# Attention in two layers of a decoder trunk: masks added, negated and reduced in one VectorE pass from PSUM into SBUF

## The chip, the core and the metric

The program runs on one core of one Trainium2 chip. A core has TensorE (PE: matmuls; PEld in the profile is its weight load), VectorE (DVE), ScalarE (ACT), GpSimd (POOL), and SyncE (SP), which here only issues DMAs. Each engine works through its own queue of instructions in order and waits on semaphores for the others. [...] The metric is device time in microseconds for one execution, the median over runs.

## What is computed

A trunk of two layers on a sequence of 1024 tokens with 1024 features, float32. Layer 0 mixes by sparse attention with 12 heads of 64 features, layer 1 by causal attention with a forget gate. Both attend with 4 more heads to 256 memory tokens, and both end with a gated convolutional feed-forward part. What matters here is the masked softmax:

```python
def masked_softmax(s, mask):
    s = jnp.where(mask, s, NEG)
    s = s - jnp.max(s, axis=-1, keepdims=True)
    e = jnp.exp(s) * mask
    return e / jnp.maximum(jnp.sum(e, axis=-1, keepdims=True), 1e-30)
```

In layer 0 each head takes three of them for every block of 128 queries: over 63 compressed keys (one for 32 tokens, every 16 tokens), over selected blocks of keys (16 of at most 16 blocks, so all of them, causally), and over a window of the last 512 keys:

```python
        p_cmp = masked_softmax(s, cmp_end[None, :] <= t[:, None])
...
        p = masked_softmax(s.reshape(B, G, HG, Q_BLOCK, n_top * L_SEL), m_sel)
...
        m_win = (s_pos[None, :] >= 0) & (s_pos[None, :] <= t[:, None]) & (t[:, None] - s_pos[None, :] < WINDOW)
        p = masked_softmax(s, m_win)
...
        return g[..., 0:1] * o_cmp + g[..., 1:2] * o_slc + g[..., 2:3] * o_win
```

In layer 1 each head takes one, over all keys up to its query. The memory heads have no mask.

## The kernel before

[...] The stages are: projections of layer 0 (to 185 us in the profile), attention of layer 0 (to 660 us), output projection, feed-forward and the projections that layer 1 needs (to about 1480 us), attention of layer 1 (to 1870 us), and again output projection and feed-forward.

**Units.** Attention goes unit by unit; a unit is one head and one half (c = 0 or 1) of the queries, four blocks of 128 (`ii` = 0 to 3, called rows here). Layer 0 has 24 such units and 8 of memory heads, layer 1 the same numbers. The selected branch and layer 1 take 128 x (4c + ii + 1) keys for a row (`causal`, line 934), so 128 to 512 columns in the first half and 640 to 1024 in the second; the window branch takes 128 to 512 in the first and 640 in the second. The 64 compressed columns are scored beside the window's (`joint`).

**One unit, engine by engine.**

- `score` (line 362, the matmuls at 385) takes a `psa` buffer, two PSUM banks or 1024 columns; there are two such buffers. A group of rows that fits in 1024 columns (`groups`) is scored at a time: for each row and each stretch of columns within a bank, two matmuls with the query block as weights. Then come the masks, also as matmuls: the weights are the identity (`identb`, bf16), the moving operand is a bf16 tile of 0 and -1e30, and PSUM adds it up. A row of the selected branch and of layer 1 has one such matmul, of 128 columns on the diagonal (`caub`). A row of the window branch has one of 192 columns (`wcb`: 128 on the diagonal and 64 compressed), and in the second half another of 128 columns at the window's far edge (`winb`).
- `maximum` (line 387) has DVE reduce each row from PSUM to its negated maximum in `stat` (line 402; 404 for the 64 compressed columns). Memory units have four equal rows and take one instruction (398).
- `exponent` (line 406) has ACT read the row from PSUM, add the negated maximum, take exp, write p to SBUF, and sum it up (418; 421 for the compressed columns, whose sum DVE takes later). p's buffer is taken here when a unit's first group comes. In layer 0 the buffers have one copy for each half and branch (`ps0`, `ps1`, `pw0`, `pw1`; `pc` has two), in layer 1 two. After it the `psa` buffer is free.
- `sums` and `clamp` (DVE 431, 433, 434; POOL 438) make the reciprocal; `normalise` scales p, by POOL in layer 0 (461, 463) and by DVE in layer 1 (465).
- Then come steps of up to four 128-wide blocks: PE transposes p into a `psb` bank (`turn_p`, 495), ACT copies the high part (`upper_p`, 506), DVE subtracts it to get the low part (`lower_p`, 509), and PE multiplies both with the values (`value`, 519). `psb` has four buffers, `pt`, the tile of the two parts, three.
- Matmuls of projections (lines 240 to 242) that later units need are put between.

**The order.** In layer 0 (`planned`, line 659) the order on every engine is made before the program is written: each piece of work is a task with an engine, a price in microseconds, tasks that it depends on, a priority, and the buffers that it takes and gives back (`Plan`, line 44). A list scheduler plays them through, and the order in which they start is the order in the queues. Priorities count in steps: transposes of step k have k, the score of a branch has the step that first needs it, less a lead of 5. The prices of a score, a maximum and an exponential are at lines 710 to 712:

```python
                        s_us += 2 * sum(map(self.columns, segs)) + 0.11 * len(br["spans"][ii][2])
                        m_us += 0.15 + 1.04e-3 * w + (0.22 if joint else 0)
                        e_us += 0.49 + 0.82e-3 * w + (0.33 if joint else 0)
```

The score takes a `psa`, and the exponential gives it back (line 718); the exponential also depends on the transposes that read the old contents of its p buffer (`old`, line 717). In layer 1 (`attention`, line 541) there is no such plan: the order comes from slots. In step k stand the maximum, then the transposes, the high part, the exponential, the low part, the normalisation, the next score and projections, each for work begun so many steps earlier.

Of the kernel before, what the change touches and what calls it, by code (L numbers as in the profile page):

```python
# [18 lines left out]
P = 128  # L19
D = 1024  # L20
S = 1024
NT = S // P
KT = D // P
CH = 512
# [4 lines left out]
NMEM = 256  # L29
# [97 lines left out]
class Trunk:  # L127
# [43 lines left out]
    def constants(self):  # L171
        nc, cp, a = self.nc, self.cp, self.a
        c = cp.tile([P, C_CAU], F32, name="consts")
        nc.sync.dma_start(c, a["consts"][:, 0:C_CAU])
        self.ident = c[:, C_ID:C_ID + P]
        self.rv = c[:, C_RV:C_RV + 1]
        self.identb = cp.tile([P, P], BF16, name="identb")
        nc.vector.tensor_copy(self.identb, self.ident)
        self.m_cau = cp.tile([P, P], BF16, name="caub")
        self.nhalf = c[:, C_NH:C_NH + 1]  # L180

    def masks(self, pool, keep):
# [3 lines left out]
        self.m_win = keep.tile([P, P], BF16, name="winb")  # L186
        nc.vector.tensor_copy(self.m_win, m[:, P:2 * P])

        self.m_wc = keep.tile([P, NT, 192], BF16, name="wcb")
        nc.vector.tensor_copy(self.m_wc[:, :, P:], m[:, 2 * P:].rearrange("p (t n) -> p t n", t=NT))  # L190
        nc.vector.tensor_copy(self.m_wc[:, :, 0:P], m[:, 0:P].rearrange("p (o n) -> p o n", o=1).to_broadcast([P, NT, P]))

    def gain(self, pool, row, bufs=1):
        g = self.sb(pool, [P, D], F32, "gb", bufs)
# [167 lines left out]
    def score(self, it):  # L362
        nc, br, s = self.nc, it["br"], self.psa()
        it["s"] = s
        for ii, o, n in it["grp"]:
            k0, k1, masks = br["spans"][ii]
            if "joint" in br:
                f, t0 = n - 192, k0 // P
                segs = [(o + f, o + n, lambda k: k[:, t0 + f // P, :])]
                if f:  # L370
                    segs.insert(0, (o, o + f, lambda k: k[:, t0:t0 + f // P, 0:P]))
            else:
                cuts = [o] + [b for b in (CH,) if o < b < o + n] + [o + n]
                segs = [(b0, b1, lambda k, b0=b0, b1=b1: k[:, k0 + b0 - o:k0 + b1 - o]) for b0, b1 in zip(cuts, cuts[1:])]
            mms = []
            for q, k in zip(br["q"], br["k"]):
                for b0, b1, at in segs:
                    rhs = at(k)
                    out = s[:, b0:b1] if len(rhs.shape) == 2 else s[:, b0:b1].rearrange("p (t n) -> p t n", n=P)
                    mms.append((b0 // CH, out, q[:, ii * P:(ii + 1) * P], rhs))  # L380
            for mo, mk in masks:
                mms.append(((o + mo) // CH, s[:, o + mo:o + mo + mk.shape[1]], self.identb, mk))
            banks = [b for b, *_ in mms]
            for i, (b, out, w, rhs) in enumerate(mms):
                nc.tensor.matmul(out, w, rhs, start=b not in banks[:i], stop=b not in banks[i + 1:])  # L385

    def maximum(self, ap, it):
        nc, br, s, grp = self.nc, it["br"], it["s"], it["grp"]
        u, joint = it["u"], br.get("joint")
        if it["first"]:  # L390
            if it["load"]:
                u["stat"] = self.sb(ap, [P, 3, 4 * len(u["branches"])], F32, "stat", 5)
            for i, b in enumerate(u["branches"]):
                b["stat"] = u["stat"][:, :, 4 * i:4 * i + 4]
        br["same"] = len({k1 - k0 for k0, k1, _ in br["spans"].values()}) == 1
        if br["same"] and len(grp) == 4:
            n = grp[0][2]
            nc.vector.reduce_max(br["stat"][:, 0, :], s[:, 0:4 * n].rearrange("p (i n) -> p i n", n=n), axis=AX.X, negate=True)
        else:
            for ii, o, n in grp:  # L400
                w = n - 64 if joint else n
                nc.vector.reduce_max(br["stat"][:, 0, ii:ii + 1], s[:, o:o + w], axis=AX.X, negate=True)  # L402
                if joint:
                    nc.vector.reduce_max(joint["stat"][:, 0, ii:ii + 1], s[:, o + w:o + n], axis=AX.X, negate=True)

    def exponent(self, ap, it):
        nc, br, s = self.nc, it["br"], it["s"]
        joint = br.get("joint")
        if it["first"]:
            for b in (br, joint) if joint else (br,):  # L410
                tag, width, bufs = b["p"]
                b["pa"], b["pt"], b["len"] = self.sb(ap, [P, width], F32, tag, bufs), {}, 0
        for ii, o, n in it["grp"]:
            w = n - 64 if joint else n
            p = br["pa"][:, br["len"]:br["len"] + w]
            br["pt"][ii] = p
            br["len"] += w
            nc.scalar.activation(p, s[:, o:o + w], AF.Exp, bias=br["stat"][:, 0, ii:ii + 1], accum_out=br["stat"][:, 1, ii:ii + 1])  # L418
            if joint:
                p = joint["pt"][ii] = joint["pa"][:, ii * 64:(ii + 1) * 64]  # L420
                nc.scalar.activation(p, s[:, o + w:o + n], AF.Exp, bias=joint["stat"][:, 0, ii:ii + 1])
                joint["len"] += 64
    def sums(self, u, i0, i1):

        nc, st = self.nc, u["stat"][:, :, 4 * i0:4 * i1]
# [233 lines left out]
    def planned(self, ap, l, od, units, works, spare, lead):  # L659
# [3 lines left out]
        pl, steps, users, oT, done = Plan(psa=2, psb=4, pt=self.n_pt, wr=3), [], {}, [], {}  # L663
# [9 lines left out]
        for w in works:  # L673
            prio = [(count + i) * n_fill / total for i in range(w["n"])]
# [8 lines left out]
        for k, u in enumerate(units):  # L683
            brs = u["branches"]
            scored = brs if len(brs) == 1 else brs[0:2]
            for br in brs:
                tag, _, bufs = br["p"]
                same = users.setdefault(tag, [])
# [7 lines left out]
            for i, br in enumerate(scored):  # L696
                due = min(st["k"] for st in u["steps"] if any(q[0] is br for q in st["ps"]))
                prio, joint, es = due - lead, br.get("joint"), []
                gs = self.groups(br)
                for j, g in enumerate(gs):  # L700
                    it = {"u": u, "br": br, "grp": g, "first": j == 0, "load": i == 0 and j == 0}
                    s_us = e_us = m_us = 0.0
                    for ii, o, n in g:
                        if joint:
                            segs = ([n - 192] if n > 192 else []) + [192]
                        else:
                            cuts = [o] + [b for b in (CH,) if o < b < o + n] + [o + n]
# [12 lines left out]
                i1 = len(brs) if br is scored[-1] else i + 1  # L720
                pool = br["on"] == "pool"
# [210 lines left out]

    @staticmethod
    def causal(c, mask):
        return {ii: (0, (c * 4 + ii + 1) * P, [((c * 4 + ii) * P, mask)]) for ii in range(4)}

    def mem_units(self, ap, qd, kv, tags, need, on):
        nc = self.nc
        kd, vd = kv
        for h in range(NMH):  # L940
            kv = {}
            for c in range(2):
                br = {"spans": {ii: (0, NMEM, []) for ii in range(4)}, "kb": P, "gate": None, "p": tags[c], "on": on}

                def load(h=h, c=c, br=br, kv=kv):
                    if c == 0:
# [243 lines left out]
    def units0(self, ap):  # L1190
        nc = self.nc
        t_s, t_w, t_c = [("ps0", 1280, 1), ("ps1", 3328, 1)], [("pw0", 1280, 1), ("pw1", 2560, 1)], ("pc", 256, 2)
        for g in range(NG):
            kk, vv = {}, {}
            vc = self.vc[:, g].rearrange("n s d -> n (s d)")
            for h in range(g * 6, g * 6 + 6):
                for c in range(2):
                    sp_c = {ii: (0, 64, []) for ii in range(4)}
                    sp_w = {}
                    for ii in range(4):  # L1200
                        i = c * 4 + ii
                        k0 = max(0, i - 4) * P
                        sp_w[ii] = (k0, (i + 1) * P, ([(0, self.m_win)] if i >= 4 else []) + [(i * P - k0, self.m_wc[:, i, :])])
# [757 lines left out]
```

## Time and profile before

| | us |
|---|---|
| median of three runs | 2640.01 |
| lowest, highest | 2638.92, 2644.44 |
| the profiled execution | 2646.97 |
| its span, first to last instruction | 2645.2 |
| stage of layer 0's attention in it | 185 to 660 |
| stage of layer 1's attention in it | 1480 to 1870 |

A row of grouped instructions reads: line, engine, operation, tile written <- tiles read, shapes, count | busy time in us, mean ns of one | idle time of the engine just before them, and what ended it. A row of the waits reads: who waited, the line and tile, whom for, us in total, times, longest. A row of windows reads: the stretch and its length, then for each engine its busy us and the count of its instructions, PE's granted clock as a share, the DMA share and the rate; asked for one line or tile, it counts only those instructions. A row of the timeline has start, duration, engine, line, operation, tiles, and the number of instructions merged in it; matmuls overlap, since a new one streams in while the last drains.

### The profile page before, as it was taken

What the parts mean: (1) busy time and instruction counts of PE and PEld (TensorE: products, weight loads), DVE (VectorE), ACT (ScalarE), POOL (GpSimd) and SP (SyncE); (2) the same over time, 40 slices, a digit from 0 to 9 for tenths busy, and PEclk for the clock granted to TensorE, in tenths of its full rate; (3) what the DMA queues carried; (4) which work ended last, traced back from release to release, by engine and by line L of the source; (5) the groups of instructions that cost most, each with busy time, mean ns of one, the idle gap of its engine ahead of it and who ended that gap; (6) DMA issues with size and microseconds to landing.
All of it is one profiled execution on the core that took longest, in us unless ns stands there. A gap on an engine that the chain in (4) does not pass through costs nothing.

```text
span 2645.2 us, 36064 instructions
## 1 busy us (share of the span) xinstructions
PE 2505.2 (95%) x12642; PEld 2074.6 (78%) x12642; DVE 1824.2 (69%) x2681; ACT 1333.6 (50%) x2553; POOL 833.2 (32%) x722
## 2 busy tenths in 40 slices
PE   7879999888999999998999999999899999998998
PEld 6768888676877888886888987787677888886886
DVE  5637776567376787877765467778466787787765
ACT  4427776677244444544454356657244544443443
POOL 1236544745143545543000000000123555454000
PEclk9989999899999999999999999999999999999999
DMA  8473233432422323337434556666532333337523
GB/s 240 137 210 100 81 91 109 115 106 81 147 88 84 104 95 104 108 133 268 134 123 132 157 176 190 188 176 179 196 112 68 104 111 101 96 105 264 189 89 119
DMA packets 302701, 357.72 MB, mean 135 GB/s; under 512 B 37960, under 2 KB 183224, under 8 KB 302520
## 3 DMA queue, kind: packets, MB, share of 16 engines
q1 hardware_dynamic: 302520, 355.41, 43.1%
q8 instruction: 100, 1.64, 0.3%
q14 instruction: 81, 0.66, 0.1%
HBM read 245.55 MB, written 109.78 MB: 134 GB/s over the span
## 4 chain that ended last, share of the span: by engine, by line
PE 74%; DVE 5%; DMA 5%; issue 4%; POOL 4%; ACT 3%; SPq 1%; POOLq 0%; ACTq 0%; DVEq 0%
PE psa L240 11%; PE psa L241 11%; PE psa L242 11%; PE psb L240 8%; PE psb L242 8%; PE psb L241 8%; PE psa L385 7%; PE psb L519 4%; PE psb L495 4%; POOL gs L1752 1%; DVE pt L509 1%; DMA hT<-in_w_down_dram 1%; ACT ps L418 1%; ACT pt L506 1%; DVE stat L402 1%
## 5 line engine op out<-in xcount | busy, mean ns | idle before, releaser
L165 ACT ACTIVATE wh<-wr 128x512 fp32r<-128x512 f32 (+2 forms) x240 | 181.9, 761 | 337.5 <-PE psb L242 143.8
L166 DVE TENSOR_TENSOR wl<-wr,wh 128x512 fp32r<-128x512 f32 (+2 forms) x232 | 223.1, 963 | 148.3 <-ACT wh L165 147.7
L1737 DVE SCALAR_TENSOR_TENSOR v<-u,cw,v 128x1023 f32<-128x1023 f32 (+1 forms) x176 | 273.2, 1552 | 68.7 <-ACT v L1735 68.5
L509 DVE TENSOR_TENSOR pt<-psb,pt 128x512 fp32r<-128x512 f32 (+2 forms) x380 | 245.4, 658 | 93.1 <-ACT pt L506 90.8
L506 ACT ACTIVATE pt<-psb 128x512 fp32r<-128x512 f32 (+2 forms) x380 | 216.8, 582 | 143.5 <-PE psb L495 97.2
L1735 ACT ACTIVATE v<-u,cw 128x1024 f32<-128x1024 f32 x88 | 109.6, 1245 | 310.3 <-DVE u L1724 283.5
L519 PE MATMUL psb<-pt,vv 128*128 128x512 f32 (+2 forms) x864 | 254.5, 372 | 4.0 <-ACT pt L506 2.2
L402 DVE TENSOR_REDUCE stat<-psa 128x1 f32<-128x640 f32 (+7 forms) x288 | 201.3, 717 | 77.8 <-PE psa L385 76.8
L240 PE MATMUL psa<-hT,wh 128*128 128x512 f32 x560 | 219.1, 392 | 5.3 <-DVE u L1698 5.3
L385 PE MATMUL psa<-kk,qq 128*128 128x512 f32 (+4 forms) x792 | 191.6, 356 | 32.2 <-DMA qq<-qd 13.3
L242 PE MATMUL psa<-hT,wl 128*128 128x512 f32 x560 | 218.5, 390 | 0.2 <-DVE wl L166 0.2
L241 PE MATMUL psa<-hT,wh 128*128 128x512 f32 x560 | 218.6, 390 | 0.0
L204 POOL TENSOR_TENSOR rs<-ss,consts 128x1 f32<-128x1 f32 x44 | 25.9, 592 | 505.0 <-DVE ss L202 366.9
L418 ACT ACTIVATE ps<-psa,stat 128x128 f32<-128x128 f32 (+2 forms) x224 | 156.1, 704 | 47.5 <-DVE stat L402 43.8
L385 PEld LDWEIGHTS psa<-kk,qq 128*128 128x128 f32 x792 | 130.7, 198 | 50.8 <-ACT ps L418 16.7
L1639 POOL TENSOR_TENSOR ws<-wr 128x512 f32<-128x512 f32 x44 | 77.5, 1761 | 294.8 <-DMA wr<-in_w_up_dram 187.5
L240 PE MATMUL psb<-hT,wh 128*128 128x512 f32 x384 | 159.6, 416 | 1.8 <-ACT wh L165 1.1
L519 PEld LDWEIGHTS psb<-pt,vv 128*128 128x128 f32 x864 | 147.1, 194 | 17.5 <-DVE pt L509 4.5
L240 PE MATMUL psb<-wh 128*128 128x512 f32 x352 | 139.4, 396 | 20.5 <-ACT wh L165 20.4
L495 PE MATMUL psb<-consts,ps 128*128 128x128 f32 x928 | 150.9, 279 | 6.7 <-POOL ps L463 3.8
L579 POOL TENSOR_TENSOR wr<-wr 128x512 f32<-128x512 f32 x16 | 20.9, 1314 | 424.6 <-DMA wr<-o 423.8
L242 PE MATMUL psb<-hT,wl 128*128 128x512 f32 x384 | 151.9, 396 | 1.1 <-POOL wl L166 1.1
(304 smaller groups left out, 6908.0 us busy)
## 6 DMA issues: line engine op xcount, KB each, us to landing
wr<-in_w_up_dram SPq DMA_DIRECT2D x88, 512.0 KB
wr<-gd SPq DMA_DIRECT2D x154, 256.0 KB
gd<-v SPq DMA_DIRECT2D x88, 256.0 KB
gd<-gs SPq DMA_DIRECT2D x66, 256.0 KB
o<-ob SPq DMA_DIRECT2D x128, 128.0 KB
wr<-o SPq DMA_DIRECT2D x32, 512.0 KB
hT<-in_w_down_dram SPq DMA_DIRECT2D x64, 256.0 KB
qd<-st SPq DMA_DIRECT2D x56, 256.0 KB
```

Of the source, the lines that this page charges most:

```text
L166: (low or nc.vector).tensor_tensor(lo, src, f32(hi), ALU.subtract)
L240: mm(out, lh, rh, start=first, stop=False, skip_group_check=more)
L241: mm(out, lh, rl, start=False, stop=False, skip_group_check=more)
L242: mm(out, ll, rh, start=False, stop=last, skip_group_check=more)
L385: nc.tensor.matmul(out, w, rhs, start=b not in banks[:i], stop=b not in banks[i + 1:])
L402: nc.vector.reduce_max(br["stat"][:, 0, ii:ii + 1], s[:, o:o + w], axis=AX.X, negate=True)
L418: nc.scalar.activation(p, s[:, o:o + w], AF.Exp, bias=br["stat"][:, 0, ii:ii + 1], accum_out=br["stat"][:, 1, ii:ii + 1])
L495: nc.tensor.transpose(tp[0:kb, x:x + P], br["pt"][ii][:, o:o + kb], self.ident)
L506: self.nc.scalar.activation(st["hi"], st["src"], AF.Copy)
L509: self.nc.vector.tensor_tensor(st["lo"], st["src"], f32(st["hi"]), ALU.subtract)
L519: self.nc.tensor.matmul(u["o"][:, iis[0] * P:iis[0] * P + w], br["v"](j), t[:, x:x + w], start=st["begin"] and first and i == 0, stop=st[" ...
L1737: nc.vector.scalar_tensor_tensor(v[:, d:], u[:, :S - d], cw[:, tap, i:i + 1], v[:, d:], ALU.mult, ALU.add)
```

## The change

1. **Masks leave PE.** `identb` is gone, and `score` writes no mask matmuls. The masks become wider bf16 tiles in SBUF, as wide as a row: `caub` is 1024 columns, 0 and then the diagonal block, and a row of n columns takes its last n; `winb` is 640 columns (far edge, 384 of 0, diagonal); a new `cmpb` holds 8 x 64 for the compressed keys. Together they take 512 bytes a partition more than before.
2. **The maximum becomes `lift`.** For a row with a mask, DVE's `tensor_tensor_reduce` reads the scores from PSUM and the mask from SBUF, writes -(s + mask) to p in SBUF, and keeps the minimum of what it writes in `stat`. That is the negated maximum as before. A row of the window branch has two of these, as it had two maxima. p's buffer is now taken here. Rows of memory units (mask `None`) stay as they were.
3. **The exponential works in SBUF, in place.** exp(-1 x p + stat), from p to p.
4. **The plan in layer 0.** The score's price loses 0.11 us for each mask. The maximum, at its old price, now depends on the readers of the old p and gives the `psa` back; the exponential depends on the maximum alone, at its old price. For memory units the exponential still gives `psa` back, but the dependence on the old p has moved to the maximum there too.

Layer 1's slots are untouched, but `maximum` and `exponent` are shared.

```diff
-        self.identb = cp.tile([P, P], BF16, name="identb")
-        nc.vector.tensor_copy(self.identb, self.ident)
-        self.m_cau = cp.tile([P, P], BF16, name="caub")
+        self.m_cau = cp.tile([P, S], BF16, name="caub")
+        nc.vector.memset(self.m_cau[:, :S - P], 0.0)
...
-        nc.vector.tensor_copy(self.m_cau, m[:, 0:P])
...
+        nc.vector.tensor_copy(self.m_cau[:, S - P:], m[:, 0:P])
+        self.m_win = keep.tile([P, 5 * P], BF16, name="winb")
+        nc.vector.memset(self.m_win[:, P:4 * P], 0.0)
...
+        self.m_cmp = keep.tile([P, NT, 64], BF16, name="cmpb")
...
-            for mo, mk in masks:
-                mms.append(((o + mo) // CH, s[:, o + mo:o + mo + mk.shape[1]], self.identb, mk))
...
+        if br["spans"][0][2] is None:
+            n = grp[0][2]
+            nc.vector.reduce_max(br["stat"][:, 0, :], s[:, 0:4 * n].rearrange("p (i n) -> p i n", n=n), axis=AX.X, negate=True)
+            return
+        for ii, o, n in grp:
+            w = n - 64 if joint else n
+            self.lift(br, ii, s[:, o:o + w])
+            if joint:
+                self.lift(joint, ii, s[:, o + w:o + n])
+
+    def lift(self, br, ii, s):
+        w = s.shape[1]
+        p = br["pt"][ii] = br["pa"][:, br["len"]:br["len"] + w]
+        br["len"] += w
+        self.nc.vector.tensor_tensor_reduce(p, s, br["spans"][ii][2], -1.0, 3e38, ALU.add, ALU.min, br["stat"][:, 0, ii:ii + 1])
...
-            nc.scalar.activation(p, s[:, o:o + w], AF.Exp, bias=br["stat"][:, 0, ii:ii + 1], accum_out=br["stat"][:, 1, ii:ii + 1])
...
+            nc.scalar.activation(p, p, AF.Exp, bias=st[:, 0, ii:ii + 1], scale=-1.0, accum_out=st[:, 1, ii:ii + 1])
...
-                        s_us += 2 * sum(map(self.columns, segs)) + 0.11 * len(br["spans"][ii][2])
+                        s_us += 2 * sum(map(self.columns, segs))
...
-                    m = pl.add("DVE", m_us, lambda it=it: self.maximum(ap, it), [s], prio)
                     old = [r for b in (br, joint) if b and b["before"] for r in reads[id(b["before"])]]
-                    es.append(pl.add("ACT", e_us, lambda it=it: self.exponent(ap, it), [m] + old, prio, (), ["psa"]))
+                    kept = br["spans"][0][2] is None
+                    m = pl.add("DVE", m_us, lambda it=it: self.maximum(ap, it), [s] + old, prio, (), () if kept else ["psa"])
+                    es.append(pl.add("ACT", e_us, lambda it=it: self.exponent(ap, it), [m], prio, (), ["psa"] if kept else ()))
```

More of the change, by code (lines that the diff above doesn't have):

```diff
@@ L365, in score @@
         for ii, o, n in it["grp"]:
-            k0, k1, masks = br["spans"][ii]
+            k0 = br["spans"][ii][0]
             if "joint" in br:
@@ L395, in maximum @@
         br["same"] = len({k1 - k0 for k0, k1, _ in br["spans"].values()}) == 1
[L396 to L408, printed above, removed]
         if it["first"]:
@@ L934, in causal @@
     def causal(c, mask):
-        return {ii: (0, (c * 4 + ii + 1) * P, [((c * 4 + ii) * P, mask)]) for ii in range(4)}
+        n = [(c * 4 + ii + 1) * P for ii in range(4)]
+        return {ii: (0, n[ii], mask[:, S - n[ii]:]) for ii in range(4)}
     def mem_units(self, ap, qd, kv, tags, need, on):
@@ L942, in mem_units @@
             for c in range(2):
-                br = {"spans": {ii: (0, NMEM, []) for ii in range(4)}, "kb": P, "gate": None, "p": tags[c], "on": on}
+                br = {"spans": {ii: (0, NMEM, None) for ii in range(4)}, "kb": P, "gate": None, "p": tags[c], "on": on}
                 def load(h=h, c=c, br=br, kv=kv):
@@ L1197, in units0 @@
                 for c in range(2):
-                    sp_c = {ii: (0, 64, []) for ii in range(4)}
+                    sp_c = {ii: (0, 64, self.m_cmp[:, c * 4 + ii, :]) for ii in range(4)}
                     sp_w = {}
```

29 lines of the change are left out of this document (16 added, 13 removed).

## The prediction

> **What bounds the kernel now.** I began with the page's first part, to see which engine is full.
>
> ```profile
> span 2645.2 us, 36064 instructions
> PE 2505.2 (95%) x12642; PEld 2074.6 (78%) x12642; DVE 1824.2 (69%) x2681; ACT 1333.6 (50%) x2553; POOL 833.2 (32%) x722
> ```
>
> TensorE (PE) is full over the whole span, VectorE (DVE) has a third of its time left. The change touches two stages only, so I asked for busy time by stretch: the attention of layer 0 runs from 185 to 660 us, that of layer 1 is at its steadiest from 1530 to 1830 us.
>
> ```profile
> core 0: us, PE busy (x) PEld busy (x) DVE busy (x) ACT busy (x) POOL busy (x), PEclk, DMA share, GB/s
> 185.00:230.00 45.00, 33.36 (x187) 26.61 (x187) 21.71 (x47) 21.89 (x54) 15.47 (x21) 0.81 0.50 123
> 230.00:480.00 250.00, 246.37 (x1616) 208.45 (x1615) 186.88 (x362) 186.21 (x467) 138.75 (x196) 1.00 0.33 92
> 480.00:660.00 180.00, 148.90 (x894) 118.08 (x894) 117.63 (x223) 124.96 (x321) 98.81 (x130) 0.92 0.38 104
> 1530.00:1830.00 300.00, 297.20 (x1665) 241.50 (x1664) 223.97 (x480) 187.61 (x474) 5.16 (x4) 1.00 0.64 182
> ```
>
> Two of these stretches are bound by PE: 230 to 480 us (246.37 of 250) and layer 1 (297.20 of 300). DVE is at 75% in both. From 185 to 230 and from 480 to 660 us PE works 182.3 of 225 us, so there it stops for others. The view of waits in layer 0 tells for whom, where scores are concerned:
>
> ```profile
> PE psa L385 <- ACT pc L421: 8.8, 9, 2.1
> PE psa L385 <- ACT ps L418: 8.1, 6, 2.2
> ACT pw L418 <- PE psb L495: 2.7, 1, 2.7
> ```
>
> PE stood 8.8 + 8.1 = 16.9 us before a score matmul because an exponential had not yet read a `psa` bank. The third row is the only time an exponential waited for the transposes that still read its output buffer.
>
> **The change, part by part.** *Masks leave PE.* 336 matmuls with `identb` as weights go, 240 in layer 0 and 96 in layer 1 (24 units of four rows).
>
> ```profile
> L385 PE MATMUL psa<-caub,identb x192: 219/230/330, 196.8 to 1851.5; 128*128 128x128 bf16 x192
> L385 PE MATMUL psa<-wcb,identb x96: 246/251/383, 203.0 to 658.3; 128*128 128x192 bf16 x96
> L385 PE MATMUL psa<-winb,identb x48: 229/230/233, 217.9 to 658.3; 128*128 128x128 bf16 x48
> ```
>
> Their 230 ns is latency in a pipelined array and not what they cost; the cost is read from start to start on PE's timeline in layer 1:
>
> ```profile
> 1786.91 0.39 PE L519 MATMUL psb<-pt,mv 128*128 128x512 f32 x1
> 1787.14 0.46 PE L385 MATMUL psa<-kk,qq 128*128 128x512 f32 x2
> ...
> 1788.60 0.23 PE L385 MATMUL psa<-caub,identb 128*128 128x128 bf16 x1
> 1788.64 0.47 PE L519 MATMUL psb<-pt,mv 128*128 128x512 f32 x1
> 1788.95 0.27 PE L495 MATMUL psb<-consts,ps 128*128 128x128 f32 x1
> ```
>
> The mask itself holds PE for 1788.64 - 1788.60 = 0.04 us. The 512 columns after it take 1788.95 - 1788.64 = 0.31 us, where the same matmul behind a long one takes 1787.14 - 1786.91 = 0.23 us: behind so short a matmul the next weights are not loaded in time. So a mask costs between 0.04 and 0.12 us. I take 0.11, near the upper end, because most masks are followed by a matmul that starts late in this way. They lie as follows (masks alone):
>
> ```profile
> 230.00:480.00 250.00, 28.12 (x137) 10.96 (x137) 0.00 (x0) 1.00 0.33 92
> 480.00:660.00 180.00, 17.44 (x80) 6.88 (x80) 0.00 (x0) 0.92 0.38 104
> 1530.00:1830.00 300.00, 19.32 (x84) 8.11 (x84) 0.00 (x0) 1.00 0.64 182
> ```
>
> In the full stretch of layer 0 that is 137 x 0.11 = 15.1 us (5.5 to 16.4), all of it on the path. The other 240 - 137 = 103 save 11.3 us of PE, but there PE is at 81% and waits on others; I credit a third, 3.8 us (0 to 11.3). Layer 1: 96 x 0.11 = 10.6 us (3.8 to 11.5).
>
> *The score banks come free earlier.* A bank was held until the exponentials had read it, now until VectorE has. The wait of 2.2 us in the rows above, engine by engine:
>
> ```profile
> 585.88 1.68 DVE L402 TENSOR_REDUCE stat<-psa 128x1 f32<-128x128 f32 x4 [1.81 <-PE psa L385]
> ...
> 587.33 0.19 ACT L418 ACTIVATION_READ_ACCUMULATOR ps<-psa,stat 128x1 f32 x1
> 587.42 0.47 ACT L418 ACTIVATE ps<-psa,stat 128x256 f32<-128x256 f32 x1
> ...
> 588.59 0.47 PE L385 MATMUL psa<-kk,qq 128*128 128x192 f32 x2 [2.22 <-ACT ps L418]
> ```
>
> All maxima of the four rows had ended by 585.88 + 1.68 = 587.56; PE was let go at 588.59. Released by VectorE it would have come at least 1.03 us sooner, about half of its 2.22. Half of 16.9 is 8.4 us (0 to 16.9).
>
> *The maximum becomes an add, a scale, a minimum and a write.* The instruction count of the maxima stays (288 in layer 0, 96 in layer 1; the memory units keep theirs); the new form reads PSUM and a mask, and writes p. The nearest rows in layer 0:
>
> ```profile
> L509 DVE TENSOR_TENSOR pt<-psb,pt 128x512 fp32r<-128x512 f32 x197 | 131.3, 682 | 43.2 <-ACT pt L506 42.6
> L402 DVE TENSOR_REDUCE stat<-psa 128x1 f32<-128x640 f32 x60 | 49.2, 821 | 26.9 <-PE psa L385 26.5
> L402 DVE TENSOR_REDUCE stat<-psa 128x1 f32<-128x512 f32 x24 | 16.3, 680 | 0.6 <-PE psa L385 0.6
> L402 DVE TENSOR_REDUCE stat<-psa 128x1 f32<-128x1024 f32 x12 | 14.6, 1220 | 6.0 <-PE psa L385 6.0
> L404 DVE TENSOR_REDUCE stat<-psa 128x1 f32<-128x64 f32 x96 | 20.5, 214 | 0.0
> L431 DVE RECIPROCAL stat<-stat 128x4 f32<-128x4 f32 x32 | 5.5, 173 | 11.6 <-ACT ps L418 7.3 <-ACT pm L418 4.3
> ```
>
> A two-input pass from PSUM and SBUF over 512 columns takes 682 ns, the reduction 680: the pass itself costs nothing more. What VectorE may need is a second step that brings the accumulator out. No such step of VectorE stands in the trace. Below, it is nothing; above, it is as long as the smallest VectorE row, 0.17 us. ScalarE's own accumulator read goes on after 587.42 - 587.33 = 0.09 us, and I take that. [...] With the read the sum is the one below, without it it would be 9.7 us lower still.
>
> Where the maxima are:
>
> ```profile
> 230.00:480.00 250.00, 76.04 (x109) 1.00 0.33 92
> 230.00:480.00 250.00, 11.99 (x56) 1.00 0.33 92
> ```
>
> 165 of the 288 lie in the full stretch: 165 x 0.09 = 14.9 us, DVE 186.9 + 14.9 = 201.7 us in 250 - 15.1 = 235, or 86%. PE still hides that, with thinner cover; I charge 4 us (0 to 15). The other 123 add 11.1 us in stretches that go by latency; a third on the path is 3.7 us. In layer 1, with one maximum for each mask, DVE comes to 223.97 + 84 x 0.09 = 231.5 of 290 us, 80%, hidden by PE; I charge 2 us.
>
> *The exponentials read SBUF.* Copies of 512 columns by ScalarE:
>
> ```profile
> L757 ACT ACTIVATE ob<-psb 128x512 f32<-128x512 f32 x31 | 18.5, 598 | 8.5 <-PE psb L519 5.7 <-DMA o<-ob 2.6
> L785 ACT ACTIVATE hT<-wr 128x512 fp32r<-128x512 f32 x14 | 8.7, 635 | 0.0
> ```
>
> SBUF costs 37 ns more. In the full stretch 165 x 0.037 = 6.1 us on an engine at 186 of 250: hidden by PE. Outside, 123 x 0.037 = 4.6, a third is 1.5 us; without its cover the first would be 6.1 more.
>
> *A wait moves.* p is now claimed by VectorE's pass instead of by the exponential, so the wait for the last transposes of the old p stands in VectorE's queue, ahead of the subtractions at L509 that PE's value matmuls need. The order in layer 0 knows this dependence, and today it is met once, 2.7 us: nothing in the sum, a rival below. The masks' own preparation at the start (a memset and casts in place of casts) is of the same few instructions under the projections: nothing.
>
> Sum: -15.1 - 3.8 - 8.4 + 4 + 3.7 + 1.5 in layer 0, -10.6 + 2 in layer 1: **-26.7 us**. The profiled execution took 2646.97 us (span 2645.2, and 1.8 around it), 7.0 above the median 2640.01. 2646.97 - 26.7 = 2620.3, so the median comes to 2613.
>
> **The rivals.** *Everything counts*: all masks (26.4 + 10.6) and all 16.9 us of bank waits come back, VectorE's additions stay hidden: -53.9, **2586**. For it: PE is full for most of the time. Against it: 103 masks lie where PE waits anyway.
>
> *VectorE takes PE's place.* If the accumulator read is not overlapped (0.17) and the new op starts 0.085 later (the RECIPROCAL's half), DVE has 186.9 + 165 x 0.255 = 229 us beside PE's 246.4 - 15.1 = 231: two full queues that feed each other, and the 250 us stay. Elsewhere -3.8 - 8.4 + 123 x 0.255 / 3 + 1.5 = -0.2, layer 1 -5.6. That is -6, **2634**, with 2622 to 2650 around it.
>
> *The pass runs at half the rate* (the slower side). Reading two streams, writing one and folding a fourth may need two cycles an element. The rate is (1220 - 821) / 384 = 1.04 ns a column. Layer 0 has 12 heads x 8960 columns (4608 selected, 3840 window, 512 compressed) = 107,500, so 112 us more on DVE; of it 64 in the full stretch: 186.9 + 64 + 14.9 = 266, some +20 there. Elsewhere 47.7 / 3 + 3.7 + 1.5 - 3.8 - 8.4 = +9; layer 1 (55,300 columns) fills DVE to 282 of 300 and gains 4. Together +25: **2665**. It decides from about a third more per column, where DVE and PE are level in the full stretch. Against it: the two-input row above runs at full rate. [...]
>
> *The new order stalls.* Layer 0 is ordered anew from prices in which VectorE's read does not appear, and VectorE may stand at the head of its queue for an old p, with L509 behind it and PE's value matmuls behind that. From 26.7 / 2.7 = 10 waits as long as the one seen, among the 24 units whose p is claimed this way, the gain is gone; in 16 of them it is 43.2 - 26.7 = +16.5: **2656**.
>
> **How the numbers follow.** Forecast 44% (its own range 2600 to 2628), everything counts 12%, VectorE as bound 22%, half rate 10%, stalls 12%. About 0.2%, 5.3 us, is what a measurement tells here, so same means 2634.7 to 2645.3. Faster: 0.43 of the forecast, 0.12, a third of the VectorE case and a tenth of the stalls, 0.64. Same: 0.01, a third of the VectorE case, a fifth of the stalls, 0.11. Slower: half rate, 0.08 of VectorE, 0.07 of the stalls, 0.25. The range runs from the full credit to just past the stalls, 2587 to 2658; the half rate is left out, and the far ends.
>
> **What would show it.** Right: no `identb` rows; the stretch that was 250 us ends some 10 us sooner with PE still over 97% and DVE near 86%; the waits of PE at L385 for ACT at L418 and L421 are gone, with shorter ones for DVE in their place; layer 1's attention is 8 or 9 us shorter. A row of VectorE's accumulator read gives the price I guessed. Wrong: the new pass over 512 columns well above 0.68 us; DVE over 93% in either stretch with PE falling; VectorE waiting for L495.

## The result, and the profile after

The changed kernel takes 2594.36 us (median of 4 runs, 2591.86 to 2596.25), the kernel before 2639.47 beside it (2638.13 to 2644.44): a ratio of 0.9825, 95% interval 0.9808 to 0.9842, so 45 us less. The forecast was 2613, with 2587 to 2658 around it: the direction holds, the gain is 18 us larger, and 2594 lies below the 2600 to 2628 that the forecast had as its own range. A second measurement in another session (e9 below) gave 0.9815 (0.9800 to 0.9831).

The stages show where it lies. Layer 0's attention is counted here from its first score matmul to its last value matmul, layer 1's likewise, each in the one profiled execution (before: 196.3 to 674.6 us and 1537.5 to 1870.8 us). A kernel that was profiled twice, below, has the same stage of layer 0 within 0.4 us.

| us | before | after | difference | the sum had |
|---|---|---|---|---|
| attention of layer 0 | 478.3 | 441.9 | -36.4 | -18.1 |
| attention of layer 1 | 333.3 | 324.2 | -9.1 | -8.6 |
| all the rest | 1833.6 | 1824.0 | -9.6 | 0 |
| span | 2645.2 | 2590.1 | -55.1 | -26.7 |

The rest, which the change hardly touches, differs by as much as the two profiled executions stand off their medians (before 7 us above, after 2.5 below); the medians differ by 45.1, the two attentions together by 45.5. So layer 1 came out in the size that was worked out, and the whole miss is in layer 0.

The first part of the page after, whole program:

```profile
span 2590.1 us, 35657 instructions
PE 2466.6 (95%) x12306; PEld 2062.5 (80%) x12306; DVE 1831.0 (71%) x3066; ACT 1339.8 (52%) x2553; POOL 832.7 (32%) x722
```

PE has 336 matmuls less (12642 to 12306), VectorE 385 instructions more (2681 to 3066), 384 of them reads of the accumulator; its busy time has risen by 7 us only. By stretch, after (busy time by engine, granted clock, DMA share):

```profile
183.00:225.00 42.00, 31.68 (x172) 27.55 (x173) 24.55 (x90) 25.02 (x66) 19.12 (x27) 0.80 0.52 137
225.00:455.00 230.00, 225.41 (x1446) 195.71 (x1445) 185.45 (x517) 186.27 (x462) 128.35 (x190) 1.00 0.32 93
455.00:635.00 180.00, 157.28 (x926) 126.94 (x926) 123.17 (x327) 132.08 (x331) 114.53 (x140) 0.97 0.39 115
1490.00:1780.00 290.00, 286.32 (x1576) 240.31 (x1574) 224.18 (x564) 190.20 (x475) 5.17 (x4) 1.00 0.64 187
```

The full stretch of layer 0 is still PE's: 225.41 of 230 us, 98%, with VectorE at 81%, not the 86% of the forecast. In the last stretch PE is busy 87% of the time, where it was 83%, at a clock of 0.97 in place of 0.92. Layer 1 is full, with VectorE at 77%.

The waits of layer 0, after, with the row that was feared as a new stall last:

```profile
PE psa L384 <- DMA qq<-qd: 11.5, 1, 11.5
PE psa L384 <- DVE stat L414: 7.8, 14, 1.2
PE psb L528 <- DVE pt L518: 4.6, 13, 0.8
...
DVE ps L414 <- PE psb L504: 1.6, 2, 0.9
```

PE no longer waits for ScalarE before a score (16.9 us before, with a longest of 2.2); in its place stand 7.8 us for VectorE, none longer than 1.2. The first row is the start of the stage. VectorE waits for transposes of an old p for 1.6 us in all.

Two rows of before's waits belong beside this, the first again the start of the stage; the second was not in the forecast's list:

```profile
PE psa L385 <- DMA qq<-qd: 13.3, 1, 13.3
PE psa L385 <- DMA qq<-qm: 9.0, 6, 5.1
```

Those 9.0 us, PE's waits for the queries of memory units, have no row after.

The new pass, in the grouped rows of layer 0's stretch after:

```profile
L414 DVE DVE_READ_ACCUMULATOR2_ANT stat<- 128x1 f32 x288 | 23.8, 83 | 0.0
L414 DVE CUSTOM_DVE_ANT_0 pc<-psa,cmpb 128x64 f32<-128x64 f32 x96 | 21.0, 219 | 0.0
L414 DVE CUSTOM_DVE_ANT_0 ps<-psa,caub 128x1024 f32<-128x1024 f32 x12 | 14.6, 1215 | 1.4 <-PE psa L384 1.4
L427 ACT ACTIVATE ps<-ps,stat 128x512 f32<-128x512 f32 x12 | 8.6, 715 | 0.0
L414 DVE CUSTOM_DVE_ANT_0 ps<-psa,caub 128x512 f32<-128x512 f32 x12 | 8.1, 671 | 0.0
```

The pass is as fast as the reduction it replaces (671 to 680 ns at 512 columns, 1215 to 1220 at 1024, 219 to 214 at 64). The exponential from SBUF takes 715 ns where it took 687 from PSUM: 28 more, 37 forecast (in the window branch it takes 716 in both kernels). And the read of the accumulator is there, 83 ns in each row. What it costs is another question, and VectorE's timeline answers it:

```profile
300.38 0.81 DVE L414 CUSTOM_DVE_ANT_0 pw<-psa,winb 128x640 f32<-128x640 f32 x1
301.12 0.08 DVE L414 DVE_READ_ACCUMULATOR2_ANT stat<- 128x1 f32 x1
301.12 0.22 DVE L414 CUSTOM_DVE_ANT_0 pc<-psa,cmpb 128x64 f32<-128x64 f32 x1
301.26 0.08 DVE L414 DVE_READ_ACCUMULATOR2_ANT stat<- 128x1 f32 x1
301.26 0.68 DVE L518 TENSOR_TENSOR pt<-psb,pt 128x512 fp32r<-128x512 f32 x1
```

And the same place in the order of before:

```profile
319.74 0.81 DVE L402 TENSOR_REDUCE stat<-psa 128x1 f32<-128x640 f32 x1
320.47 0.21 DVE L404 TENSOR_REDUCE stat<-psa 128x1 f32<-128x64 f32 x1
```

The next instruction starts in the same hundredth of a microsecond as the read, 0.74 us after the pass of 640 columns began; before it was 320.47 - 319.74 = 0.73. The read lies beside the next instruction and holds up nothing that these rows can show. Over the whole program 317 of the 384 instructions behind a read start within 15 ns of it.

### The profile page after: what moved, and what is told of

Read it like the earlier page. It is cut to its first block, busy times and chain, and to the rows that moved or that the text cites. A ratio compares the mean times of both kernels' runs of the same rounds, so it can differ in the third digit from the quotient of the medians.

```text
span 2590.1 us, 35657 instructions
## 1 busy us (share of the span) xinstructions
PE 2466.6 (95%) x12306; PEld 2062.5 (80%) x12306; DVE 1831.0 (71%) x3066; ACT 1339.8 (52%) x2553; POOL 832.7 (32%) x722
## 4 chain that ended last, share of the span: by engine, by line
PE 72%; DVE 6%; DMA 6%; ACT 5%; POOL 4%; issue 2%; SPq 1%; POOLq 0%; ACTq 0%; DVEq 0%
PE psa L241 11%; PE psa L242 11%; PE psa L243 11%; PE psb L241 8%; PE psb L243 8%; PE psb L242 8%; PE psa L384 4%; PE psb L528 4%; PE psb L504 4%; POOL gs L1763 1%; DMA hT<-in_w_down_dram 1%; ACT pt L515 1%; DVE pt L518 1%; DVE ps L414 1%; ACT ps L427 1%
## 5 line engine op out<-in xcount | busy, mean ns | idle before, releaser
L1748 DVE SCALAR_TENSOR_TENSOR v<-u,cw,v 128x1023 f32<-128x1023 f32 (+1 forms) x176 | 282.8, 1607 | 68.7 <-ACT v L1746 67.1
L528 PE MATMUL psb<-pt,vv 128*128 128x512 f32 (+2 forms) x864 | 244.6, 361 | 12.6 <-DVE pt L518 7.0
L384 PE MATMUL psa<-kk,qq 128*128 128x512 f32 (+4 forms) x792 | 181.8, 349 | 23.8 <-DMA qq<-qd 11.8
L205 POOL TENSOR_TENSOR rs<-ss,consts 128x1 f32<-128x1 f32 x44 | 25.8, 589 | 503.6 <-DVE ss L203 365.3
L414 DVE CUSTOM_DVE_ANT_0 ps<-psa,caub 128x128 f32<-128x128 f32 (+1 forms) x192 | 138.9, 750 | 42.0 <-PE psa L384 37.3
L427 ACT ACTIVATE ps<-ps,stat 128x128 f32<-128x128 f32 (+1 forms) x192 | 147.5, 771 | 31.6 <-DVE stat L414 31.4
L1650 POOL TENSOR_TENSOR ws<-wr 128x512 f32<-128x512 f32 x44 | 68.6, 1559 | 290.3 <-DMA wr<-in_w_up_dram 255.4
```

Of the source, the lines that this page charges most:

```text
L427: nc.scalar.activation(p, p, AF.Exp, bias=st[:, 0, ii:ii + 1], scale=-1.0, accum_out=st[:, 1, ii:ii + 1])
L528: self.nc.tensor.matmul(u["o"][:, iis[0] * P:iis[0] * P + w], br["v"](j), t[:, x:x + w], start=st["begin"] and first and i == 0, stop=st[" ...
L1748: nc.vector.scalar_tensor_tensor(v[:, d:], u[:, :S - d], cw[:, tap, i:i + 1], v[:, d:], ALU.mult, ALU.add)
```

## The experiments

What is open is where another 18 us of layer 0 came from. Three readings stood against each other: the masks were worth more than they were credited with; VectorE's additions, charged with 7.7 us in layer 0, cost nothing because VectorE has cover; or the earlier release of the score banks, in the order and on the chip, is worth more than half of PE's waits for ScalarE. Eleven runs were made, one of them the kernel after again and one a repetition. The times of before beside them are 2642.27 us for e1 to e4, 2644.18 for e5 to e8 and 2648.62 for e9 to e11, so ratios are compared.

**Masks alone, out of the kernel before (e1), and the order made anew without them (e2).**

```diff
-            for mo, mk in masks:
-                mms.append(((o + mo) // CH, s[:, o + mo:o + mo + mk.shape[1]], self.identb, mk))
```

> The kernel before without its mask matmuls (scores stay unmasked, so this leaves the masks out of the computation), in the order of before. Theory 1, masks are what PE was full with, at 0.11 us each everywhere: 240 + 96 masks, 37 us, 2602. As the prediction credited them (a third outside the full stretch): 15.1 + 3.8 + 10.6 = 29.5 us, 2610. Theory 2, the early release of the banks and the new order are most of the gain: masks give under 20 us, 2620 or more.

2614.33 us (2611.47 to 2621.35), ratio 0.9902 (0.9885 to 0.9919). In the profiles layer 0's attention goes from 478.3 to 464.0, -14.3, layer 1's from 333.3 to 323.8, -9.5. That is 0.06 us for each of the 240 masks in layer 0, and 0.10 for each of the 96 in layer 1. PE's waits before a score are still there:

```profile
PE psa L383 <- DMA qq<-qm: 10.4, 6, 4.7
PE psa L383 <- ACT ps L416: 7.8, 6, 2.3
PE psa L383 <- ACT pc L419: 7.5, 8, 1.2
```

So the masks alone don't bring the result, and they bring back only 1.6 of the 16.9 us of waits for ScalarE. The first reading falls: 14.3 us in layer 0 is less than the 18.9 that the sum credited. The time lies between the 2610 of that credit and the 2620 of theory 2.

```diff
-                        s_us += 2 * sum(map(self.columns, segs)) + 0.11 * len(br["spans"][ii][2])
+                        s_us += 2 * sum(map(self.columns, segs))
```

> As the run before, with the 0.11 us a mask taken out of the plan too, so layer 0 is ordered anew without masks. If the order has no part of its own: within 4 us of the run before. If a new order by itself moves layer 0 by much, 10 us or more to either side, and layer 1 stays as in the run before.

e2 has this edit on top of e1: 2608.80 us (2606.72 to 2612.86), 0.9879 (0.9865 to 0.9894), layer 0 in 460.3. A plan that knows that the masks are gone brings 3.7 us more by the profile; the intervals of the two ratios overlap.

**The masks put back into the kernel after (e3),** as matmuls of zeros, as many and as wide; order and VectorE pass are those of after.

```diff
...
+            if br["spans"][0][2] is not None:
+                w = n - 64 if "joint" in br else n
+                for mo, mw in ([(0, P)] if "joint" in br and w == 5 * P else []) + [(w - P, 192 if "joint" in br else P)]:
+                    mms.append(((o + mo) // CH, s[:, o + mo:o + mo + mw], self.identb, self.m_cau[:, S - P - mw:S - P]))
```

> The changed kernel in its own order, with as many matmuls by the identity put back on PE at the same places (of zeros, so the result is unchanged). Theory 1: the gain of 45 us falls by 37 us, to about 2631. Prediction's credit: by 29.5, 2624. Theory 2: under 20 us, below 2614.

2614.17 us (2612.16 to 2622.37), 0.9908 (0.9889 to 0.9927). Layer 0 takes 454.5, 12.6 more than after, layer 1 331.1, 6.9 more. With its gain cut by 20 us it stands at the edge of theory 2 and short of the credit's 2624. In layer 0 the masks (-14.3 by e1) and everything else (478.3 to 454.5, -23.8) add up to -38.1, where both together gave -36.4: two nearly separate gains, and the masks are the smaller one. Over both layers they are the larger: 14.3 + 9.5 = 23.8 of 45.5 us.

**VectorE loaded with more work (e4, e7).** If VectorE has cover in layer 0, more work of the size of the read should cost little.

```diff
...
+        for _ in range(2):
+            self.nc.vector.tensor_copy(self.idle[:, 0:4], self.ident[:, 0:4])
```

> The changed kernel with two copies of 4 columns on VectorE behind each of the 384 new passes, about 0.085 us each from start to start, 0.17 us together: the upper price that the prediction had for the accumulator read. If VectorE's time counts as the prediction charged it (9.7 us for 0.09 a pass): about 18 us slower, 2612. If PE covers VectorE wholly: within 5 us of 2594. If VectorE is next to be the bound: over 30 us slower.

2727.52 us (2721.62 to 2735.45), 1.0329 (1.0306 to 1.0351); layer 0 in 577.7 us, 135.8 more. As a probe of VectorE's cover it failed, since the copies are not what they were meant to be. First their row in layer 0, then their busy time in and behind it:

```profile
L417 DVE COPY idle<-consts 128x4 f32<-128x4 f32 x609 | 174.3, 286 | 10.7
```

```profile
194.00:771.70 577.70, 173.90 (x607) 0.90 0.28 79
771.70:830.00 58.30, 29.43 (x162) 1.00 0.47 162
```

A copy of four columns takes 286 ns on average in layer 0 and 29.43 / 162 = 0.18 us behind it. The timelines of VectorE and of GpSimd (POOL) show where the long ones lie:

```profile
242.73 0.37 DVE L417 COPY idle<-consts 128x4 f32<-128x4 f32 x2
245.60 0.73 DVE L417 COPY idle<-consts 128x4 f32<-128x4 f32 x2
```

```profile
244.35 0.24 POOL L450 TENSOR_SCALAR stat<-stat 128x8 f32<-128x8 f32 x1 [5.58 <-DVE stat L443]
244.69 2.37 POOL L475 TENSOR_SCALAR pw<-pw,stat,gates 128x128 f32<-128x128 f32 x4
```

At 242.73 GpSimd is idle, and two copies take 0.37 us; at 245.60 it normalises p, and two take 0.73. Of all 768 copies the 549 that started with GpSimd idle took 168 ns on average and 173 at most; the 219 that started inside a GpSimd instruction took 507 on average and up to 2275. What holds such a copy back no run shows. How much of the 135.8 us is those long copies and how much the rest of VectorE's added time isn't separated here: VectorE is busy for 475.0 us in this stage, 332.2 after.

So the probe was made again with a memset, which reads nothing:

```diff
...
+        self.nc.vector.memset(self.idle, 0.0)
```

> The changed kernel with a VectorE memset of 144 columns behind each of the 384 passes, which reads nothing and so has no part in what the copies of the earlier run met with GpSimd; about 0.12 to 0.18 us each. If VectorE's time counts as the prediction charged it (9.7 us for 0.09): 13 to 19 us slower, about 2610. If PE covers VectorE: within 5 us of 2594. If the 133 us of the earlier run were VectorE's time and no contention: over 80 us slower.

2610.92 us (2607.60 to 2612.87), 0.9875 (0.9860 to 0.9890).

```profile
L416 DVE MEMSET idle<- 128x144 f32 x306 | 54.5, 178 | 2.1
```

Layer 0 takes 457.5, 15.6 more than after. VectorE's busy time in it has risen from 332.2 to 365.3 by the rows of the whole stage:

```profile
191.80:649.30 457.50, 419.90 (x2540) 352.28 (x2541) 365.34 (x1235) 347.20 (x855) 260.54 (x354) 0.97 0.35 100
```

```profile
193.00:634.90 441.90, 414.23 (x2539) 350.07 (x2540) 332.19 (x929) 343.32 (x855) 260.64 (x354) 0.98 0.35 104
```

15.6 of 33.1 is 0.47 us of the stage for each microsecond that VectorE works longer. So a memset that the plan doesn't know of is paid for in layer 0, about half: VectorE is not covered there, and the second reading falls: the pass costs nothing because it takes no longer, not because something hides it. Of layer 1 the run says nothing: its 78 remaining memsets ran before that stage.

**The earlier release of the banks, taken apart (e5, e6).** In e5 the plan is told that the exponential gives the banks back, as before; on the chip they come free behind VectorE all the same.

```diff
-                    kept = br["spans"][0][2] is None
+                    kept = True
```

> The changed kernel, but in layer 0's plan the exponential gives the score bank back, as before; on the chip the bank is still free once VectorE has read it. So only the order differs from the changed kernel. Theory A, the order that the early release allows is what the pass brings beyond the masks: layer 0's attention goes back to about 460 us, as in the reordered run without masks (442 in the changed kernel), so about 2612. Theory B, the release on the chip is what counts: within 5 us of 2594.

In e6 the exponential also reads the scores from PSUM again, so that the banks are held until it has; VectorE's pass is the same, and p is claimed by it. Its masks are zeros.

```diff
...
-            nc.scalar.activation(p, p, AF.Exp, bias=st[:, 0, ii:ii + 1], scale=-1.0, accum_out=st[:, 1, ii:ii + 1])
+            w = n - 64 if joint else n
+            nc.scalar.activation(p, s[:, o:o + w], AF.Exp, bias=st[:, 0, ii:ii + 1], accum_out=st[:, 1, ii:ii + 1])
...
```

> As the run before, and the exponential reads the scores from PSUM again (the masks are zeros here, so the result leaves them out of the computation), so the chip holds the bank until then too. VectorE's pass and the missing mask matmuls stay. Theory A: the same as the run before within 5 us. Theory B: 15 us or more slower than that, about 2612. Either way layer 1 within 3 us of the changed kernel's 323.

e6: 2611.78 us (2608.41 to 2613.87), 0.9877 (0.9860 to 0.9893), layer 0 in 458.1. e5: 2603.05 us (2602.25 to 2605.54), 0.9848 (0.9833 to 0.9863), layer 0 in 448.0. Neither theory holds alone: 2603 lies between the 2612 of one and the 2594 of the other, and e6 is 8.7 us slower than e5, where one said within 5 and the other 15 or more. Layer 1 takes 325.5 in e6, 1.3 more than after. PE's waits before a score, e6 and then e5, with the row for GpSimd's normalised p last:

```profile
PE psa L384 <- ACT ps L428: 10.0, 5, 3.1
PE psa L384 <- ACT pc L431: 9.3, 7, 1.7
PE psa L384 <- DMA qq<-qm: 4.3, 2, 3.8
PE psb L505 <- POOL ps L473: 1.0, 3, 0.4
```

```profile
PE psa L384 <- DMA qq<-qm: 5.6, 5, 3.8
PE psa L384 <- DVE stat L414: 3.7, 6, 0.9
PE psb L504 <- POOL ps L472: 8.9, 18, 2.1
```

With the VectorE pass and the banks held as before, PE waits 19.3 us for ScalarE, and the stage is within 2.2 us of e2, which has no masks either, the old maximum, and the same order on PE. The release on the chip, at the same order as e6, turns 19.3 us into 3.7 and takes 10.1 off the stage. The difference isn't all gain, since PE now waits 8.9 us for GpSimd in place of 1.0. That the plan knows of the release, and orders by it, takes off 448.0 - 441.9 = 6.1 more, and the wait for GpSimd is down to 2.6 us there; the times agree in direction (0.9848 to 0.9825 and 0.9815), though their intervals overlap.

**The plan's prices (e8 to e11).** The order still goes by the old prices of the maximum and the exponential. e8 gives them what the profile after shows from start to start:

```diff
-                        m_us += 0.15 + 1.04e-3 * w + (0.22 if joint else 0)
-                        e_us += 0.49 + 0.82e-3 * w + (0.33 if joint else 0)
+                        m_us += (0.02 if m_us else 0.1) + 0.06 + 1.04e-3 * w + (0.145 if joint else 0)
+                        e_us += (0.0 if e_us else 0.14) + 0.285 + 0.83e-3 * w + (0.24 if joint else 0)
```

> The changed kernel with the plan's prices of a maximum and an exponential set to what the trace shows from start to start (VectorE 0.06 + 1.04e-3 a column and 0.145 for the compressed columns; ScalarE 0.285 + 0.83e-3 a column and 0.24), both lower than the plan has. If prices close to the chip's make a better order: 5 to 15 us faster than 2594. If the order goes by luck at this level: within 10 us to either side.

2589.37 us (2587.76 to 2593.20), 0.9797 (0.9782 to 0.9812), layer 0 in 433.6. Since this is near the spread, after and e8 were measured again side by side, together with prices that err to the other side:

> The changed kernel unaltered, as the reference for the next two on the same chip: 2594 within 4 us.

> The kernel with measured prices once more. If its lead of 5 us is more than chance between sessions: 3 to 8 us under the run before, with layer 0's attention near 434 us. If not: within 2 us of it.

```diff
-                        m_us += 0.15 + 1.04e-3 * w + (0.22 if joint else 0)
-                        e_us += 0.49 + 0.82e-3 * w + (0.33 if joint else 0)
+                        m_us += 0.22 + 1.04e-3 * w + (0.295 if joint else 0)
+                        e_us += 0.69 + 0.82e-3 * w + (0.42 if joint else 0)
```

> The changed kernel with the same two prices wrong the other way: a maximum 0.07 dearer, an exponential 0.20 dearer than the plan has. If the order gains by prices that are nearer to the chip's: 3 to 15 us slower than the changed kernel. If the order goes by luck: as likely faster as slower, within 10 us.

| | us | ratio to before | layer 0's attention |
|---|---|---|---|
| e9, after | 2598.10 (2594.26 to 2601.92) | 0.9815 (0.9800 to 0.9831) | 441.7 |
| e10, measured prices | 2590.66 (2587.51 to 2593.92) | 0.9788 (0.9773 to 0.9803) | 434.0 |
| e11, prices raised | 2600.56 (2597.81 to 2604.01) | 0.9826 (0.9811 to 0.9841) | 446.2 |

No run of e10 is as slow as the fastest of e9, and both profiles of either kernel agree on the stage within 0.4 us: measured prices are worth some 7 us, and this version beats both kernels. Raised prices cost 4.5 us in one profile of the stage; by the times e11 and e9 can't be told apart. That prices nearer to the chip's make better orders in general is not shown: 7 us lies inside the 10 that a lucky order was allowed, and the raised prices, at 2.5 us, cost less than the 3 to 15 expected.

## Why the prediction was right, and where its sizes were off

The direction and the main mechanisms held, and the size did not. Some 18 us below the forecast, 2594 is 8 us from the rival "everything counts" (2586), and it is inside the stated 2587 to 2658 only because that range was drawn down to the rival's full credit. Layer 0, put together from the profiles, each step against the terms of the sum that it answers to:

| step | us | from | the sum had |
|---|---|---|---|
| masks leave PE, old order | -14.3 | before, e1 | -15.1 - 3.8 |
| order made without them | -3.7 | e1, e2 | 0 |
| VectorE pass, banks still held | -2.2 | e2, e6 | +4 + 3.7 |
| banks free on the chip, exponential from SBUF | -10.1 | e6, e5 | -8.4 + 1.5 |
| the plan knows it | -6.1 | e5, after | with the row above |
| all | -36.4 | | -18.1 |

*Masks.* The mechanism held; 0.11 us was nearly right for layer 1 (0.10 by e1, though 0.07 by e3) and too much for layer 0 as a whole (0.06 by e1, 0.05 by e3), although two thirds of the masks outside the full stretch had been left out. The interval of 0.04 to 0.12 held both. In all, 23.8 us came in place of 29.5. The weights that come late behind a mask stand on the timeline of weight loads, for the matmuls that the forecast compared, the one at 1786.91 behind a long matmul and the one at 1788.64 behind a mask:

```profile
1786.68 0.19 PEld L519 LDWEIGHTS psb<-pt,mv 128*128 128x128 f32 x1
1788.60 0.20 PEld L519 LDWEIGHTS psb<-pt,mv 128*128 128x128 f32 x1
```

The first load ends 0.04 us before its matmul starts, the second 0.16 us after.

*VectorE's accumulator read was mis-sized.* That VectorE has such a step was an assumption, which no row of before shows. The second instruction stands in the trace after, and its row of 83 ns matches the 0.09 that was taken. But the 0.09 was charged as time in which VectorE does nothing else, and the timeline shows 0.01 from start to start. The value had been read off ScalarE, where the next instruction did start 0.09 later. That was 7.7 us in layer 0 and 2 in layer 1, the "9.7 us lower still" that the forecast named for a free read. The rate at which it was charged was not too high: 7.7 of 26 us, 0.30, against 0.47 in e7.

*The release of the banks was mis-sized.* The half had been read off one wait, of 2.22 us, of which the early release would have spared "at least" 1.03. At one and the same order (e6 to e5) the release turned PE's 19.3 us of waits for ScalarE into 3.7 for VectorE, so four fifths went, though 7.9 us of new waits for GpSimd took the place of some; before against after it looks like half, 16.9 us for ScalarE and 7.8 for VectorE, because the order differs too. -16.2 came in place of -8.4 + 1.5, the slower exponential included. 10.1 of it is the release on the chip and 6.1 the order that the plan makes with it, and two things beside the waits for the banks can be named, of which one is shown in part. PE's 9.0 us for the queries of memory units are gone after; they had not left when only the masks went (10.4 in e1) nor when the plan held the banks late (4.3 and 5.6), so they hang on the order, but which loads moved was not taken apart. And with the long waits a slower clock goes. The longest of them within the stage of before, on PE's timeline, and the stretches around it:

```profile
484.85 0.55 PE L385 MATMUL psa<-mk,qq 128*128 128x256 f32 x1 [5.11 <-DMA qq<-qm]
```

```profile
478.00:480.40 2.40, 1.74 (x15) 1.43 (x13) 1.74 (x2) 2.40 (x7) 2.40 (x3) 1.00 0.48 102
480.40:485.60 5.20, 0.55 (x1) 0.29 (x1) 1.76 (x5) 1.67 (x8) 3.95 (x7) 0.67 0.86 265
485.60:489.00 3.40, 3.33 (x14) 3.02 (x15) 1.31 (x2) 0.18 (x1) 0.71 (x2) 0.51 0.77 198
489.00:492.00 3.00, 3.00 (x20) 2.48 (x19) 1.38 (x2) 2.56 (x9) 0.22 (x1) 1.00 0.27 66
```

PE stops for 5.11 us, the clock drops during the stop, and for 3.4 us after it PE works at 0.51 before the clock is full again. In shorter stretches the stop looks like this:

```profile
480.40:482.00 1.60, 0.00 (x0) 0.00 (x0) 1.56 (x5) 1.60 (x8) 0.43 (x2) 1.00 1.01 374
482.00:482.50 0.50, 0.00 (x0) 0.00 (x0) 0.20 (x1) 0.07 (x1) 0.42 (x1) 0.62 0.77 176
482.50:485.60 3.10, 0.55 (x1) 0.29 (x1) 0.00 (x0) 0.00 (x0) 3.10 (x5) 0.50 0.81 223
```

PE had stopped at 484.85 - 5.11 = 479.74, so the clock was full for 2.26 us of the stop and stood at 0.50 before 2.76 of it were over. A stop of 2.22 us, a wait for a bank, was also followed by it:

```profile
509.25 0.60 PE L385 MATMUL psa<-kk,qq 128*128 128x192 f32 x2 [2.22 <-ACT ps L418]
```

```profile
509.40:512.80 3.40, 3.40 (x16) 3.28 (x17) 0.82 (x4) 0.46 (x2) 2.54 (x5) 0.50 0.98 288
```

Behind the equally long wait that the prediction shows, at 588.59, the clock stayed at 1.00 (588.60 to 592.00), so the price of such a wait is not its length alone. The whole of layer 0 in e6, e5 and e8:

```profile
193.90:652.00 458.10, 420.75 (x2539) 356.08 (x2540) 333.61 (x930) 339.88 (x856) 258.98 (x354) 0.96 0.35 100
```

```profile
196.10:644.10 448.00, 414.99 (x2539) 349.63 (x2540) 333.26 (x930) 347.20 (x857) 258.03 (x354) 0.98 0.36 102
```

```profile
192.10:625.70 433.60, 409.42 (x2539) 346.29 (x2540) 332.67 (x929) 343.09 (x853) 256.45 (x351) 0.99 0.36 105
```

The same 2539 matmuls keep PE busy for 420.75 us at 0.96, 414.99 at 0.98 and 409.42 at 0.99: of the 10.1 us between e6 and e5, 5.8 are busy time of PE, not waits. A slower clock was not a term of the sum.

*The order.* That a new order is worth anything by itself was in the sum only as a danger. It was a gain three times, 3.7 (e2), 6.1 (e5 to after) and 8 (e8), and a loss of 4.5 once (e11).

*Layer 1.* -9.1 against -8.6, but through two errors that cancel in part: the masks alone gave 9.5, not 10.6, and the read was nothing, not 2.

*The rivals.* "Everything counts" (2586) was nearest in time, nearer than the forecast, and half right in mechanism: of the waits for the banks nearly all came back (16.2 of 16.9 us, through the order and the clock as well), but only 23.8 of the masks' 37.0, a new order added 3.7 that it did not have, and VectorE's additions were nothing because the pass takes no longer, not because PE hides them. VectorE as the bound and the half rate needed a longer pass; it takes 671 ns for 680. The half rate's "some +20" in the full stretch would be +16 by its own 266 us; nothing hangs on it. The stall on an old p came to 1.6 us in two waits for the transposes.

*What was to show it.* No mask matmuls, the waits for ScalarE replaced by shorter ones for VectorE, PE above 97% in the full stretch, layer 1 some 9 us shorter: all found; the full stretch ended 25 us sooner (455 for 480), not 10. VectorE at 86% was not found, by the read.

## What to carry to other kernels

An instruction's row says how long it lasted, not what it costs (the read: 83 ns in its row, 0.01 us from start to start): take the price from start to start, on the engine in question, and distrust a price borrowed from another engine. Giving a shared buffer back earlier, with a plan that knows of it, was worth nearly all of the waits that named it here (16.2 us for 16.9 before), since the order and PE's clock moved with them (0.97 over layer 0's attention before, 0.98 after); counting half of those waits gave half of what came. After a change to the work, try the planner with the measured prices: here that was worth some 7 us more, in one order.

## What the runs showed of the hardware that was not expected

- A copy of 4 float32 columns within SBUF on VectorE took 168 ns (at most 173) when GpSimd was idle as it started, and 507 ns (at most 2275) when it started inside a GpSimd instruction. A memset of 144 columns in the same place took 178 ns every time, and the new pass, from PSUM and a bf16 mask, was as fast as the reduction (671 ns for 680 at 512 columns).
- The new pass shows the read of its accumulator as a row of 83 ns, and 317 of the 384 next instructions started within 15 ns of it; 288 of these reads left VectorE's busy time in layer 0 where it was (334.1 us before, 332.2 after).
- From e6 to e8, with other waits and another order, PE's busy time for the same 2539 matmuls went from 420.75 to 409.42 us, and the granted clock from 0.96 to 0.99. In the kernel before, a stop of PE of 5.11 us and one of 2.22 were followed by 3.4 us at 0.51 and 0.50, and another of 2.22 by 3.4 us at 1.00.
